# Experts' passes in another order, first gather by halves, last w2 and scatter by quarters, final mean on all partitions, one more prefetch tile

## The chip, the cores and the metric

One core of a Trainium2 chip runs the whole network. The metric is the time of one execution on the device in microseconds (us); lower is better. The engines are TensorE (PE, with its weight load PEld), VectorE (DVE), ScalarE (ACT), GpSimd (POOL) and SyncE (SP), whose queue issues nearly all transfers.

## The reference

256 tokens of width 1024 in float32 go through two blocks. Only the end of the second is touched here: a mixture of 32 experts, of which each token takes two, then a last norm and modulation.

```python
def hier_moe(h, w_rg, b_rg, w_re, b_re, w1e, w3e, w2e):
    pg = jax.nn.softmax((t @ w_rg + b_rg).astype(f32), axis=-1)
    pg_top, g_idx = lax.top_k(pg, 1)
    le = (t @ w_re + b_re).astype(f32).reshape(-1, N_GROUPS, EXPERTS_PER_GROUP)
    le_sel = jnp.take_along_axis(le, g_idx[:, :, None], axis=1)[:, 0]
    pe = jax.nn.softmax(le_sel, axis=-1)
    pe_top, e_idx = lax.top_k(pe, TOP_K)
    ...
    for e in range(N_EXPERTS):
        he = jax.nn.silu(t @ w1e[e]) * (t @ w3e[e])
        out = out + cw[:, e:e + 1] * (he @ w2e[e])
...
        x = x + gt2[:, None, :] * hier_moe(h2, ...)
    shf, scf = jnp.split(c_act @ w_ada_f + b_ada_f, 2, axis=-1)
    return modulate(rmsnorm_2(x, g_final), shf, scf)
```

## The kernel before

Activations lie with features on partitions: `x[0]` to `x[7]` are 128 features x 256 tokens each. The weights of all 32 experts are read, 96 MB in all: per expert two 1 MB halves of `w13` (512 input features each, w1 and w3 side by side) and 1 MB of `w2e`. Every load is one tile `we` of 128x2048 floats, issued by SP in the order of `expert_list` (L1838).

**The ring.** `expert_ring` collects 18 tiles from several pools: two `wa`, nine `we` (`NAHEAD`), three `s`, one `xl` and three `wf`, of which the later ones come free only when earlier stages are done with them. Load i takes the tile of load i-18, and SP issues loads strictly in order: a load whose tile is still read holds all that stand behind it. `expert_ahead` issues the 18 first loads as soon as their tiles are free. Loads of passes' experts below `NFIX` are of fixed experts; others read the expert's number from `moe_idx` (L1854), which the router's counts give, sorted so that the experts with most tokens come early.

**The passes.** `PASSES` (L41) lists eleven: six of two experts with 64 token slots each, then five of four experts with 32. One pass is `up` (tokens times `w13`, in two halves h), `mid` (transposes), `down` (times `w2e`) and, one pass later, `scatter` into four PSUM banks. `gather` picks the tokens of two passes at a time with one-hot matmuls out of `hhi`, `hlo` (tokens on partitions) into eight tiles `gT`. `moe_round` runs gather 0, the turn of the sort (`turn`), `up(0)`, `place`, and then for each n `up(n+1)`, `mid(n)`, `scatter(n-1)`, `down(n)`. The list of loads follows that only in part: it has `dn[2]` ahead of `up[3]`, while PE does `up(3)` ahead of `down(2)`.

**The start.** `post2` feeds the mean of squares of the tokens (`sums_tok`, matmuls with `mean1`); `moe` turns it into the scale `rt` (`rsqrt_tok`: add on DVE, power -0.5 on POOL), makes the router's choice in some thirty small DVE operations, counts slots with matmuls of `moe_msk`, builds the one-hots `oh` and starts gather 0. `keep_warm` puts matmuls on PE whose result nobody reads.

**The end.** The last pass's four `w2e` tiles come in two halves each (L1862), the first halves of all four first. After the last scatter `xr` (the residual x) takes up the sums, ACT squares it (`sq`), matmuls with `mean1` give the mean per token on partitions (128x2), DVE and POOL turn it into `rte`, four matmuls with the identity (`con`) spread it over all partitions (`bcast`, L444), and eight multiplies and eight modulations give `o`, which SP stores in five pieces.

Of the kernel before, what the change touches and what calls it, by code (L numbers as in the profile page):

```python
# [42 lines left out]
X_POOL, X_ORDER, X_ADD = (1, 2), (0, 3, 1, 2, 4, 5, 6, 7), (4, 6)  # L43
X_LOADS = (0, 1), (2, 3, 4), (5, 6, 7), ()
WARM = 40, 14
NEARLY = 2
NAHEAD = 9
# [134 lines left out]
class Net:  # L182
# [49 lines left out]
    def mm(self, out, lhsT, rhs, start=True, stop=True):  # L232
        self.nc.tensor.matmul(out, lhsT, rhs, start=start, stop=stop, skip_group_check=True)  # L233
# [26 lines left out]
    def setup(self):  # L260
# [29 lines left out]
        nc.vector.memset(self.mean1, 1.0 / D)  # L290
        self.ones = self.cst.tile([P, P], BF, name="ones")
        nc.gpsimd.memset(self.ones, 1.0)
        self.mhalf = self.cst.tile([P, 32], F32, name="mhalf")
        nc.gpsimd.memset(self.mhalf, -0.5)
# [137 lines left out]
    def sums_tok(self, srcs, out, start=True):  # L432
        for i, src in enumerate(srcs):
            for j in range(2):
                self.mm(out[:, j:j + 1], src[:, j * P:(j + 1) * P], self.mean1, start and i == 0 and j == 0, i == len(srcs) - 1)

    def rsqrt_tok(self, src, eps, n, tag="rt"):
        t = self.tmp(tag + "t", (P, n))
        e = self.tmp(tag + "e", (P, n))
        self.ts(t, src, eps, op0=OP.add)  # L440
        self.tt(e, t, self.mhalf[:, :n], OP.pow, eng=self.nc.gpsimd)
        return e
# [618 lines left out]
    def block2_in(self):  # L1061
# [13 lines left out]
        self.tt(e12, m3, self.mhalf[:, :2], OP.pow, eng=nc.gpsimd)  # L1075
# [23 lines left out]
    def block2(self, post):  # L1099
        nc, A = self.nc, self.A  # L1100
        rest = self.block2_in()
        with self.tc.tile_pool(name="b2", bufs=1, reuse_waits="tile") as bp:
# [50 lines left out]
            self.sums_tok(self.acc["n"][:2], self.pr[:, 128:130], False)  # L1153
# [424 lines left out]
    def moe_pre(self):  # L1578
# [13 lines left out]
        self.ei, self.e4 = T("ei", (P, 1)), T("e4", (P, 4))  # L1592
        tm = self.tmp("t3")[:, 0:P].rearrange("p (q e) -> p q e", e=32)
# [32 lines left out]
    def keep_warm(self, n):  # L1626

        p, a = self.spare
        for _ in range(n):
            self.mm(p[:, :S], a[:, 0:P], a)  # L1630

    def moe(self, final):
        nc, A = self.nc, self.A
        pr = self.pr
        self.sums_tok(self.acc["n"][2:], pr[:, 128:130], False)
# [6 lines left out]
        with self.tc.tile_pool(name="moe", bufs=1, reuse_waits="tile") as mp:  # L1642
# [61 lines left out]
            self.keep_warm(WARM[0])  # L1704
# [5 lines left out]
            self.mm(pk[:, 64:96], self.ones, mk[:, 32:64], False, True)  # L1710
            self.keep_warm(WARM[1])
# [3 lines left out]
            self.rk, self.cw = self.rc[:, 0:2], self.rc[:, 2:4]  # L1715
# [4 lines left out]
            def low(g, j):  # L1720
                c = slice(g * 512, (g + 1) * 512)
                self.stt(self.hlo[j][:, c], self.pt[g][j], rt[:, j:j + 1], self.hhi[j].bitcast(F32)[:, c], op0=OP.mult, op1=OP.subtract)
# [6 lines left out]
            self.tt(self.rk.rearrange("p a b -> p (a b)"), pk[:, 0:64], big, OP.add)  # L1729
# [5 lines left out]
            self.yl = self.wl.tile([P, D], F32R, tag="l", name="yl")  # L1735

            es = ExitStack()
            es.enter_context(self.tc.issue_after(picked.ins))
            gd, ge = t(2, 4), t(2, 4)
            self.tt(gd, lg, bc(gm, 4), OP.subtract)  # L1740
            self.act(ge, gd, AF.Exp)
            gs = red(ge, (2,), OP.add)
            d12, ds = t(8), t(2, 4)
            self.tt(d12, m2, m1, OP.subtract)
            self.tt(f2(ds), d12, f2(ohg), OP.mult)
            d1 = red(ds, (2,), OP.add)
            e2, dn, dn2, w1, w2 = t(2), t(2), t(2), t(2), t(2)
            self.act(e2, d1, AF.Exp)
            self.ts(dn, e2, 1.0, op0=OP.add)
            self.tt(dn2, dn, gs, OP.mult)  # L1750
            nc.vector.reciprocal(w1, dn2)
            self.tt(w2, w1, e2, OP.mult)
            for j in range(2):
                a = t(32)
                c = slice(32 * j, 32 * j + 32)
                self.ts(a, f2(o1m)[:, c], w1[:, j:j + 1], op0=OP.mult)
                self.stt(self.cw[:, j], f2(o2m)[:, c], w2[:, j:j + 1], a)
            cm = red(pk[:, 64:96], (1,))
            th, nx = t(3), t(1)
            for i in range(3):  # L1760
                self.ts(th[:, i:i + 1], cm, 64 * (i + 1) + 0.5, op0=OP.is_gt)
            order = self.expert_order(T, pk[:, 64:96])
            tn = t(3)
            for i in range(3):
                self.ts(tn[:, i:i + 1], self.top8[:, NWIDE - NFIX:NWIDE - NFIX + 1], 1024 * (i + 1) + 0.5, op0=OP.is_gt)
            self.tt(th, th, tn, OP.max)
            nc.vector.tensor_reduce(nx, th, axis=AX.X, op=OP.add)
            nxi = T("nxi", (P, 1), I32)
            nc.vector.tensor_copy(nxi, nx)
            es.close()  # L1770

            self.moe_round(*order)
            final()
            n_more = nc.values_load(nxi[0:1, 0:1], min_val=0, max_val=3)
            with self.tc.For_i(0, n_more, 1):
                self.ts(self.rk, self.rk, -64.0, op0=OP.add)
                for c, cap in ((slice(0, NWIDE), 64.0), (slice(NWIDE, NEXP), 32.0)):
                    a = self.rcP[:, 0:2, c]
                    self.ts(a, a, -cap, op0=OP.add)
                self.one_hot(0)  # L1780
                self.moe_round()
                final()

    def expert_order(self, T, cnt):
# [7 lines left out]
        rcT = rcT[:, 0:P]  # L1792
        ex = T("ex", (P, 32), BF)
# [5 lines left out]
        w = self.tmp("t2")  # L1799
# [9 lines left out]
        def turn():  # L1809
            self.po = self.bank("p1")  # L1810
# [27 lines left out]
    def expert_list(self):  # L1838
# [35 lines left out]
    def one_hot(self, b):  # L1874

        of = PASSES[2 * b:2 * b + 2]
        p0, n, cap = of[0][0], sum(q[1] for q in of), of[0][2]
        rk = self.rcP[:, 0:2] if b else self.rk
        self.oh[b] = [self.ptmp(f"oh{j}", (P, S), F32R, bufs=2) for j in range(2)]
        for j in range(2):  # L1880
            last = self.tt(self.oh[b][j][:, :n * cap].rearrange("p (e s) -> p e s", s=cap), self.C("iota")[:, 0:cap].unsqueeze(1).to_broadcast([P, n, cap]),
                           rk[:, j, p0:p0 + n].unsqueeze(2).to_broadcast([P, n, cap]), OP.is_equal)
        return last

    def moe_round(self, turn=lambda: None, place=lambda: None):
# [3 lines left out]
        ohs, gTs, hes, mids = self.oh, {}, {}, {}  # L1889

        def gather(b):
# [4 lines left out]
            gT = gTs[b] = [self.xp.tile([P, S], F32, tag=f"xh{k}", name=self.name("gT")) for k in range(KD)]  # L1896
            for dd in range(4):
# [6 lines left out]
                self.act(gT[2 * dd][:, :w], pg[:, 0:w], AF.Identity, bias=self.M(3)[:, 2 * dd:2 * dd + 1])  # L1904
                self.ts(gT[2 * dd + 1][:, :w], pg[:, S:S + w], self.M(3)[:, 2 * dd + 1:2 * dd + 2], op0=OP.add)

        def up(n):

            gT, (p, m, cap) = gTs[n // 2], PASSES[n]
            ph = self.bank("p1")  # L1910
            for h in range(2):
                w = self.expert_get(*[(0, p + i, h) for i in range(m)])
                for k in range(4):
                    for i in range(m):
                        c = n % 2 * P + i * cap
                        self.mm(ph[i * cap:(i + 1) * cap, :], gT[4 * h + k][:, c:c + cap], w[i][:, k * 512:(k + 1) * 512], h == 0 and k == 0, h == 1 and k == 3)
            s, he = self.tmp("t0"), self.tmp("t1")
            self.act(s, ph[:, 0:S], AF.Silu)
            self.tt(he, s, ph[:, S:2 * S], OP.mult)
            hes[n] = he  # L1920
# [268 lines left out]
```

## Time and profile before

| | us |
|---|---|
| median of 3 runs | 1623.12 (1621.87 to 1624.07) |
| the profiled execution | 1623.47 |
| its span | 1621.6 |

| engine | busy us | share of the span |
|---|---|---|
| PE | 1540.0 | 95% |
| PEld | 1360.5 | 84% |
| DVE | 1049.3 | 65% |
| ACT | 697.2 | 43% |
| POOL | 321.3 | 20% |

The profile is of one execution; its time is 1.9 us above its span and 0.35 us above the median. The chain of work that ended last is 76% PE over the whole span, but that is a mean over stages: the experts' stage takes the last sixth, and there the DMA engines move about 420 GB/s. The page shows the span in 40 slices; the rows of the experts' stage are those from about 1355 us on.

### The profile page before, as it was taken

The page shows a single profiled execution, that of the slowest core. Times are in us where ns is not written, and L with a number is a line of the kernel's source. Part 1 is how long each engine was busy: PE and PEld are TensorE (multiplying, and loading weights), DVE is VectorE, ACT ScalarE, POOL GpSimd, SP SyncE. Part 2 cuts the span into 40 slices and gives each one's busy share as a digit, 9 for nine tenths or more (in the row PEclk, how much of TensorE's full clock was granted, in tenths as well). Part 3 has the DMA queues.
Part 4 walks back from the last instruction along what each step waited for, and adds up shares of the span by engine and source line. Part 5 has one row for each costly group of instructions (what it writes and reads, how often), then busy time and mean ns, then how long its engine had stood idle before and what let it go on. Part 6 is the DMA issues. An engine that isn't in the chain of part 4 may idle for free.

```text
span 1621.6 us, 29873 instructions
## 1 busy us (share of the span) xinstructions
PE 1540.0 (95%) x11888; PEld 1360.5 (84%) x11888; DVE 1049.3 (65%) x1932; ACT 697.2 (43%) x1240; POOL 321.3 (20%) x340
## 2 busy tenths in 40 slices
PE   8999998999999999999999999998999989999885
PEld 8999996789999999999779999998889888454322
DVE  6777777776775577766986777757784576222112
ACT  6544444545444445444554445534464433111002
POOL 4122222132221112211222221224212031000000
PEclk9999999999999999999999999999999999999997
DMA  8676554135764567654324775543441087889993
GB/s 303 247 276 205 189 205 166 53 124 206 268 228 166 205 222 270 221 176 169 134 104 157 259 261 211 180 153 118 143 148 53 27 292 305 322 335 420 421 421 133
DMA packets 61330, 344.33 MB, mean 212 GB/s; under 512 B 11008, under 2 KB 15232, under 8 KB 27392
## 3 DMA queue, kind: packets, MB, share of 16 engines
q1 hardware_dynamic: 58368, 340.65, 57.0%
q0 software_dynamic: 640, 1.57, 0.4%
q8 instruction: 95, 1.56, 0.4%
q10 hardware_dynamic: 2176, 0.13, 0.1%
q14 instruction: 51, 0.42, 0.1%
HBM read 339.05 MB, written 2.36 MB: 211 GB/s over the span
## 4 chain that ended last, share of the span: by engine, by line
PE 76%; DVE 8%; DMA 8%; issue 3%; POOL 2%; ACT 2%; SPq 0%; ACTq 0%; DVEq 0%; POOLq 0%
PE ps L233 75%; DMA we<-in_w 5%; DMA we<-in_w2e 2%; DVE l L239 2%; PE ps L236 1%; ACT h L258 1%; DVE t L239 1%; POOL rte L239 1%; DVE xl L248 1%; DVE xh L243 0%; POOL t L239 0%; DMA s<-in_ev_win 0%; DVE t L248 0%; POOL sq L239 0%; POOL kne L239 0%
## 5 line engine op out<-in xcount | busy, mean ns | idle before, releaser
L233 PE MATMUL ps<-xh,h 128*128 128x256 f32 x1992 | 570.0, 286 | 12.3 <-ACT h L258 7.5
L233 PE MATMUL ps<-xh,l 128*128 128x256 f32 x1992 | 569.5, 286 | 0.2 <-DVE l L239 0.2
L233 PE MATMUL ps<-xl,h 128*128 128x256 f32 x1992 | 568.8, 286 | 0.3
L258 ACT ACTIVATE h<-s 128x1024 fp32r<-128x1024 f32 (+4 forms) x419 | 401.7, 960 | 368.4 <-PE ps L233 288.9
L239 DVE TENSOR_TENSOR l<-s,h 128x1024 fp32r<-128x1024 f32 (+4 forms) x416 | 465.3, 1126 | 140.9 <-ACT h L258 139.5
L233 PEld LDWEIGHTS ps<-xh,h 128*128 128x128 f32 x1992 | 380.0, 191 | 17.1 <-ACT h L258 6.8
L233 PEld LDWEIGHTS ps<-xh,l 128*128 128x128 f32 x1992 | 380.1, 191 | 5.9 <-DVE l L239 2.0
L233 PEld LDWEIGHTS ps<-xl,h 128*128 128x128 f32 x1992 | 380.4, 191 | 1.7 <-DVE xl L248 1.1
L233 PE MATMUL ps<-ah,h 128*128 128x256 f32 x704 | 201.4, 286 | 0.0
L239 POOL TENSOR_TENSOR t<-t,t 128x256 f32<-128x256 f32 x93 | 120.4, 1294 | 399.4 <-DVE t L239 339.0
L233 PE MATMUL ps<-ah,l 128*128 128x256 f32 x704 | 199.3, 283 | 0.1
L233 PE MATMUL ps<-al,h 128*128 128x256 f32 x704 | 199.1, 283 | 0.0
L233 PEld LDWEIGHTS ps<-ah,l 128*128 128x128 f32 x704 | 134.9, 192 | 0.4 <-DVE l L239 0.3
L233 PEld LDWEIGHTS ps<-al,h 128*128 128x128 f32 x704 | 135.0, 192 | 0.0
L233 PEld LDWEIGHTS ps<-ah,h 128*128 128x128 f32 x704 | 134.9, 192 | 0.0
L233 PE MATMUL ps<-we,gT 128*32 128x512 f32 (+1 forms) x512 | 100.6, 620 | 10.1 <-DMA we<-in_w 9.7
L239 DVE TENSOR_TENSOR t<-ps,rb 128x256 f32<-128x256 f32 x196 | 81.9, 421 | 32.5 <-PE ps L233 24.8
L258 ACT ACTIVATE ah<-t 128x256 fp32r<-128x256 f32 x88 | 36.7, 417 | 115.5 <-POOL t L239 115.5
L233 PEld LDWEIGHTS ps<-we,gT 128*32 128x32 f32 (+1 forms) x512 | 26.7, 124 | 66.1 <-issue 46.0
L239 DVE TENSOR_TENSOR al<-t,ah 128x256 fp32r<-128x256 f32 x88 | 38.0, 431 | 62.9 <-ACT ah L258 62.9
L248 DVE SCALAR_TENSOR_TENSOR ada<-s,ca,ada 128x1024 f32<-128x1024 f32 x56 | 71.5, 1277 | 0.0
L239 POOL TENSOR_TENSOR sa<-sa,sq 128x256 f32<-128x256 f32 x34 | 41.8, 1231 | 149.9 <-ACT sq L258 149.4
(484 smaller groups left out, 2100.5 us busy)
## 6 DMA issues: line engine op xcount, KB each, us to landing
s<-in_ffn_gu SPq DMA_DIRECT2D x87, 1024.0 KB
we<-in_w SPq DMA_DIRECT2D x64, 1024.0 KB
s<-in_ffn_dn SPq DMA_DIRECT2D x64, 704.0 KB
we<-in_w2e SPq DMA_DIRECT2D x28, 1024.0 KB
s<-in_w_ada SPq DMA_DIRECT2D x24, 1024.0 KB
s<-in_w_in SPq DMA_DIRECT2D x18, 1024.0 KB
s<-in_w_ada_f SPq DMA_DIRECT2D x8, 1024.0 KB
s<-in_ev_win SPq DMA_DIRECT2D x7, 1024.0 KB
```

The costliest lines, as they stand in the source:

```text
L233: self.nc.tensor.matmul(out, lhsT, rhs, start=start, stop=stop, skip_group_check=True)
L236: self.nc.tensor.transpose(out, in_, ident)
L239: return (eng or self.nc.vector).tensor_tensor(out, a, b, op=op)
L248: self.nc.vector.scalar_tensor_tensor(out, a, s, b, op0=op0, op1=op1)
L258: self.nc.scalar.activation(out, a, f, **kw)
```

## The change

1. `PASSES` alternates: (0, 2, 4, 6) of two experts, (12, 16) of four, 8, 20, 10, 24, 28. `expert_list` now follows PE's order throughout: `up[n+1]`, then `dn[n]`. `NFIX` is 8 instead of 6.
2. `NAHEAD` is 10 instead of 9: 19 tiles in the ring. `dynamic_dma_scratch_size=8192` frees the memory. The two first expert loads are issued some 100 us earlier, beside loads of `w_in`.
3. The router: the last mean of squares is summed before the router's own matmuls of the last tile; slots are counted with one more matmul (`pre_skip`), so that `oh` is built straight from PSUM against `slots`, without the two steps `t<-moe_msk` and `moe_rc<-ps,t`. The fillers of `keep_warm` are 26 and 5 (and 6 new ones at the end) instead of 40 and 14.
4. Gather 0 is cut in halves: four `gT`, the first half of `up(0)`, the other four, the rest of `up(0)`. The sort and the weights' exponentials come after it.
5. The last `down` goes by quarters: its `w2e` tiles come in four pieces each (16 of 256 KB), and down, scatter and residual follow quarter by quarter. `w2e` is laid out for that in memory.
6. The final mean: eight matmuls of `mean1` broadcast with `sq` (128x256) leave the mean of squares on all partitions; DVE adds the epsilon, POOL takes the power -0.5 of all 128x256 values (`t1<-t0,mhalf`), and the multiplies read that. The two adds of squares on DVE, the two residual adds on POOL, and the spreading matmuls with `rte` are gone. `mhalf` is one column, broadcast.

```diff
-NFIX, NWIDE = 6, 12
-PASSES = [(p, 2, 64) for p in range(0, NWIDE, 2)] + [(p, 4, 32) for p in range(NWIDE, NEXP, 4)]
+NFIX, NWIDE = 8, 12
+PASSES = [(p, 2 if p < NWIDE else 4, 64 if p < NWIDE else 32) for p in (0, 2, 4, 6, 12, 16, 8, 20, 10, 24, 28)]
...
-WARM = 40, 14
+WARM = 26, 5, 6
-NAHEAD = 9
+NAHEAD = 10
...
-            self.sums_tok(self.acc["n"][:2], self.pr[:, 128:130], False)
+            self.summed = self.sums_tok(self.acc["n"], self.pr[:, 128:130], False)
...
             self.mm(pk[:, 0:64], us, mk)
+            self.mm(pk[:, 0:64], self.skip, mk, False, False)
...
-            big = t(64)
-            self.ts(big, mk, -1.0e6, 1.0e6, op0=OP.mult, op1=OP.add)
...
-            self.tt(self.rk.rearrange("p a b -> p (a b)"), pk[:, 0:64], big, OP.add)
             picked = self.one_hot(0)
...
-        return up[0] + up[1] + dn[0] + up[2] + dn[1] + dn[2] + up[3] + sum((u + d for u, d in zip(up[4:], dn[3:])), []) + dn[-1]
+        return up[0] + sum((u + d for u, d in zip(up[1:], dn)), []) + dn[-1]
...
-                for c in range(2):
+                for c in range(4):
                     for o, a in self.late:
-                        self.nc.sync.dma_start(o[:, c * D:(c + 1) * D], a[:, c * D:(c + 1) * D])
+                        self.nc.sync.dma_start(o[:, c * 512:(c + 1) * 512], a[:, c * 512:(c + 1) * 512])
...
-        gather(0)
+        gather(0, (0, 1))
+        up_half(0, 0)
+        gather(0, (2, 3))
+        turn, place = early() if early else (lambda: None, lambda: None)
         turn()
-        up(0)
+        up_half(0, 1)
         place()
...
-            down(n)
-        scatter(N - 1)
...
+            if n < N - 1:
+                down(n)
+        w = None
+        for q in range(5):
+            if q < 4:
+                w, last = down(N - 1, q * 256, (q + 1) * 256, w)
+            if q:
+                with self.tc.issue_after(last.ins):
+                    scatter(N - 1, (2 * q - 2, 2 * q - 1))
+                for d in (2 * q - 2, 2 * q - 1):
+                    self.stt(self.x[d], acc[q - 1][:, (d % 2) * S:(d % 2 + 1) * S], self.M(5)[:, d:d + 1], self.x[d])
...
-        for k in X_ADD:
-            self.tt(sq[k], sq[k], sq[k + 1], OP.add)
-        self.sums_tok([q for k, q in enumerate(sq) if k - 1 not in X_ADD], p)
-        pb = self.bcast(self.rsqrt_tok(p[:, :2], EPS, 2), "p0")
+        with self.tc.issue_after(self.downed.ins):
+            for k in range(KD):
+                self.mm(p[:, :S], self.mean1.to_broadcast([P, P]), sq[k], k == 0, k == KD - 1)
+        ms, r = self.tmp("t0"), self.tmp("t1")
+        self.ts(ms, p[:, :S], EPS, op0=OP.add)
+        self.tt(r, ms, self.mhalf.to_broadcast([P, S]), OP.pow, eng=self.nc.gpsimd)
...
-            self.tt(ok, self.x[k], pb[:, :S], OP.mult)
+            self.tt(ok, self.x[k], r, OP.mult)
...
-    nc = bacc.Bacc("TRN2", target_bir_lowering=False, num_devices=1)
+    nc = bacc.Bacc("TRN2", target_bir_lowering=False, num_devices=1, dynamic_dma_scratch_size=8192)
```

On PE, at the end of gather 0, before: the last gather matmul (`hlo`), the two matmuls of the sort, and the first half of `up(0)` (`we,gT`), whose eight matmuls read the two first tiles of the ring.

```order
L233 MATMUL ps_17011<-oh_3167_16916,hlo_16908 128x256
L233 LDWEIGHTS ones
L233 MATMUL ps_17022<-moe_ex,ones 128x32
L236 MATMUL ps_17022<-con,moe_rc 128x128
L233 MATMUL ps_17027<-we_15207,gT_16970 64x512
L233 MATMUL ps_17027<-we_15209,gT_16970 64x512
```

The same place now, after the sixteenth gather matmul of thirty-two:

```order
L233 MATMUL ps_16930<-oh_3168_16898,hlo_16891 128x256
L233 MATMUL ps_16941<-we_15207,gT_16911 64x512
L233 MATMUL ps_16941<-we_15209,gT_16911 64x512
L233 MATMUL ps_16941<-we_15207,gT_16912 64x512
L233 MATMUL ps_16941<-we_15209,gT_16912 64x512
L233 MATMUL ps_16941<-we_15207,gT_16913 64x512
L233 MATMUL ps_16941<-we_15209,gT_16913 64x512
L233 MATMUL ps_16941<-we_15207,gT_16914 64x512
L233 MATMUL ps_16941<-we_15209,gT_16914 64x512
L233 MATMUL ps_16950<-oh_3167_16897,hhi_16888 128x256
```

The first half of `up(0)` moved ahead of half of the gather and ahead of the sort's two matmuls.

On SP's queue, before, the last loads that need no index, and the first that read `moe_idx` (load 18, which takes the tile of load 0):

```order
L1864 DMA we_16808<-in_w2e 128x2048
L1864 DMA we_16810<-in_w2e 128x2048
L1864 DMA we_16812<-in_w2e 128x2048
L1854 TENSOR_LOAD moe_idx
L1854 ISA x2
L1864 ISA
L1864 DMA we_17223<-in_w 128x2048
```

The same place now:

```order
L1874 DMA we_16818<-in_w 128x2048
L1874 DMA we_17212<-in_w 128x2048
L1874 DMA we_17313<-in_w2e 128x2048
L1874 DMA we_17315<-in_w2e 128x2048
L1864 TENSOR_LOAD moe_idx
L1864 ISA x2
L1874 ISA
L1874 DMA we_17332<-in_w 128x2048
```

There were 18 loads ahead of the first index; now there are 22, and of these the last three (`we_17212`, `we_17313`, `we_17315`) reuse tiles.

On PE, at the end of the program, before: the last scatter, the means per token, and the spreading of `rte`.

```order
L233 MATMUL ps_16969<-t_3449_18677,yh 128x256
L233 MATMUL ps_16969<-t_3449_18677,yl 128x256
L233 MATMUL ps_18795<-mean_170,sq_18804 128x1 x2
L233 MATMUL ps_18795<-mean_170,sq_18808 128x1 x2
L233 MATMUL ps_18830<-con,rte_18827 128x128 x2
```

The same place now:

```order
L233 MATMUL ps_16910<-t_3448_18624,yh 128x256
L233 MATMUL ps_16910<-t_3448_18624,yl 128x256
L233 MATMUL ps_18768<-yh 128x256 x6
L233 MATMUL ps_18775<-sq_18776,mean_170 128x256
L233 MATMUL ps_18775<-sq_18778,mean_170 128x256
L233 MATMUL ps_18775<-sq_18780,mean_170 128x256
```

Five more of that kind follow. Eight wide matmuls (after six fillers) stand where the small means stood, and PE has nothing to do after the power any more.

## Rows read from the trace of the kernel before

**Rows 1.** Busy by stretch: start:end, length, engines' busy time (instructions), clock, DMA share, GB/s.

```profile
1440.00:1590.00 150.00, 133.36 (x800) 57.15 (x800) 30.50 (x75) 17.54 (x33) 0.00 (x0) 0.98 1.01 420
```

**Rows 2.** The chain that ended last, the experts' passes: start, length, what.

```profile
1411.44 0.59 PE ps L236 x4
...
1441.44 0.58 PE ps L236 x4
...
1482.99 20.12 DMA we<-in_w
```

**Rows 3.** Busy by stretch of 5 us, up to where transfers are steady.

```profile
1355.00:1360.00 5.00, 5.00 (x45) 5.00 (x44) 0.84 (x2) 0.42 (x1) 0.15 (x1) 1.00 0.45 187
...
1370.00:1375.00 5.00, 3.82 (x27) 3.19 (x27) 4.93 (x28) 2.87 (x6) 0.00 (x0) 1.00 0.43 180
1375.00:1380.00 5.00, 2.92 (x16) 1.43 (x17) 3.41 (x18) 1.76 (x2) 0.00 (x0) 0.86 0.00 0
...
1425.00:1430.00 5.00, 5.00 (x43) 4.79 (x41) 2.45 (x7) 1.90 (x4) 0.00 (x0) 1.00 0.57 236
1430.00:1435.00 5.00, 5.00 (x29) 2.28 (x29) 2.58 (x7) 0.98 (x2) 0.00 (x0) 1.00 0.00 0
```

**Rows 4.** SP's queue in order of time: start, time from first to last, loads.

```profile
1360.08 4.16 SPq L1864 DMA_DIRECT2D we<-in_w2e  x4
1383.78 12.23 SPq L1864 DMA_DIRECT2D we<-in_w  x8
...
1417.55 1.58 SPq L1864 DMA_DIRECT2D we<-in_w2e  x2
1434.60 5.97 SPq L1864 DMA_DIRECT2D we<-in_w  x8
```

**Rows 5.** Busy by stretch of 2 us, where the last weights land.

```profile
1590.00:1592.00 2.00, 1.98 (x15) 0.39 (x7) 0.06 (x1) 0.69 (x1) 0.00 (x0) 1.00 0.69 279
```

**Rows 6.** Instructions in order of time, router and first gather: start, length, [idle before].

```profile
1360.78 0.42 ACT L258 ACTIVATE sq<-xr 128x256 f32<-128x256 f32 x1 [3.06 <-DVE xr L248]
...
1362.72 0.50 PE L233 MATMUL ps<-mean,sq 128*128 128x1 f32 x4
...
1369.28 0.76 DVE L239 TENSOR_TENSOR oh<-con,moe_rc 128x256 fp32r<-128x256 f32 x2
...
1378.03 0.18 PE L233 MATMUL ps<-moe_ex,ones 32*128 32x32 bf16 x1 [2.08 <-DVE moe_ex L243]
...
1378.40 8.78 PE L233 MATMUL ps<-we,gT 128*64 128x512 f32 x32
...
1387.99 7.09 PE L233 MATMUL ps<-we,gT 128*64 128x512 f32 x32 [0.38 <-DVE moe_rcP L1818]
```

**Rows 7.** Instructions in order of time, from the last down to the output.

```profile
1598.83 1.90 PE L233 MATMUL ps<-we,t 128*32 128x512 f32 x10
...
1600.83 0.69 ACT L258 ACTIVATE yh<-ps,cs 128x512 fp32r<-128x512 f32 x1 [3.74 <-PE ps L233]
...
1603.02 1.66 DVE L248 SCALAR_TENSOR_TENSOR xr<-ps,mod,xr 128x256 f32<-128x256 f32 x4 [0.71 <-PE ps L233]
1603.53 1.59 ACT L258 ACTIVATE sq<-xr 128x256 f32<-128x256 f32 x4 [2.02 <-DVE xr L248]
...
1609.22 2.74 DVE L239 TENSOR_TENSOR o<-xr,ps 128x256 f32<-128x256 f32 x8 [2.10 <-PE ps L233]
```

**Rows 8.** POOL by tile (min/median/max ns) and, last, by line (busy, mean ns).

```profile
L239 POOL TENSOR_TENSOR rte<-rtt,mhalf x10: 687/722/1787, 18.2 to 1607.2; 128x2 f32<-128x2 f32 x10
L239 POOL TENSOR_TENSOR kne<-knt,mhalf x4: 1007/1266/1985, 1105.4 to 1164.9; 128x4 f32<-128x4 f32 x4
...
L239 POOL TENSOR_TENSOR xr<-t,xr x2: 727/730/732, 1594.5 to 1595.6; 128x256 f32<-128x256 f32 x2
...
L1375 POOL COPY rw_wc<-W 128x4 f32<-128x4 f32 x4 | 1.6, 397 | 1.4 <-ACT W L258 1.4
```

**Rows 9.** Busy by stretch, where the two first expert loads go now.

```profile
1095.00:1100.00 5.00, 5.00 (x44) 5.00 (x43) 2.06 (x3) 2.35 (x4) 4.08 (x8) 1.00 0.39 127
```

More of the change, by code (lines that the diff above doesn't have):

```diff
@@ L232, in mm @@
     def mm(self, out, lhsT, rhs, start=True, stop=True):
-        self.nc.tensor.matmul(out, lhsT, rhs, start=start, stop=stop, skip_group_check=True)
+        return self.nc.tensor.matmul(out, lhsT, rhs, start=start, stop=stop, skip_group_check=True)
     def tr(self, out, in_, ident):
@@ L434, in sums_tok @@
             for j in range(2):
-                self.mm(out[:, j:j + 1], src[:, j * P:(j + 1) * P], self.mean1, start and i == 0 and j == 0, i == len(srcs) - 1)
+                last = self.mm(out[:, j:j + 1], src[:, j * P:(j + 1) * P], self.mean1, start and i == 0 and j == 0, i == len(srcs) - 1)
+        return last
     def rsqrt_tok(self, src, eps, n, tag="rt"):
+        e = self.tmp(tag + "e", (P, n))
         t = self.tmp(tag + "t", (P, n))
-        e = self.tmp(tag + "e", (P, n))
         self.ts(t, src, eps, op0=OP.add)
-        self.tt(e, t, self.mhalf[:, :n], OP.pow, eng=self.nc.gpsimd)
+        self.tt(e, t, self.mhalf.to_broadcast([P, n]), OP.pow, eng=self.nc.gpsimd)
         return e
@@ L1629, in keep_warm @@
         for _ in range(n):
-            self.mm(p[:, :S], a[:, 0:P], a)
+            last = self.mm(p[:, :S], a[:, 0:P], a[:, 0:S])
+        return last
     def moe(self, final):
@@ L1703, in moe @@
             mk = f2(msk)
-            self.keep_warm(WARM[0])
+            with self.tc.issue_after(self.summed.ins):
+                self.keep_warm(WARM[0])
             pk = self.bank("p1")
@@ L1747, in moe @@
[L1747 to L1767, printed above, removed]
@@ L1768, in moe, with weights @@
-            nxi = T("nxi", (P, 1), I32)
-            nc.vector.tensor_copy(nxi, nx)
-            es.close()
-            self.moe_round(*order)
+            nxi = T("nxi", (P, 1), I32)
+            def weights():
+                es = ExitStack()
+                es.enter_context(self.tc.issue_after(picked.ins))
+                self.ts(self.rc[:, 0:2].rearrange("p a b -> p (a b)"), pk[:, 0:64], BIG, op0=OP.add)
+                cm = red(pk[:, 64:96], (1,))
+                order = self.expert_order(T, pk[:, 64:96])
+                gd, ge = t(2, 4), t(2, 4)
+                self.tt(gd, lg, bc(gm, 4), OP.subtract)
+                with self.tc.issue_after(self.gathered.ins):
+                    self.act(ge, gd, AF.Exp)
+                gs = red(ge, (2,), OP.add)
+                d12, ds = t(8), t(2, 4)
+                self.tt(d12, m2, m1, OP.subtract)
+                self.tt(f2(ds), d12, f2(ohg), OP.mult)
+                d1 = red(ds, (2,), OP.add)
+                e2, dn, dn2, w1, w2 = t(2), t(2), t(2), t(2), t(2)
+                with self.tc.issue_after(self.gathered.ins):
+                    self.act(e2, d1, AF.Exp)
+                self.ts(dn, e2, 1.0, op0=OP.add)
+                self.tt(dn2, dn, gs, OP.mult)
+                nc.vector.reciprocal(w1, dn2)
+                self.tt(w2, w1, e2, OP.mult)
+                for j in range(2):
+                    a = t(32)
+                    c = slice(32 * j, 32 * j + 32)
+                    self.ts(a, f2(o1m)[:, c], w1[:, j:j + 1], op0=OP.mult)
+                    self.stt(self.cw[:, j], f2(o2m)[:, c], w2[:, j:j + 1], a)
+                th, nx, tn = t(3), t(1), t(3)
+                for i in range(3):
+                    self.ts(th[:, i:i + 1], cm, 64 * (i + 1) + 0.5, op0=OP.is_gt)
+                    self.ts(tn[:, i:i + 1], self.top8[:, NWIDE - NFIX:NWIDE - NFIX + 1], 1024 * (i + 1) + 0.5, op0=OP.is_gt)
+                self.tt(th, th, tn, OP.max)
+                nc.vector.tensor_reduce(nx, th, axis=AX.X, op=OP.add)
+                nc.vector.tensor_copy(nxi, nx)
+                es.close()
+                return order
@@ L1773, in moe @@
+            self.moe_round(weights)
+            self.spare = self.bank("p1"), self.yh
+            with self.tc.issue_after(self.scattered.ins):
+                self.keep_warm(WARM[2])
             final()
@@ L1895, in gather @@
             w = P * len(PASSES[2 * b:2 * b + 2])
-            gT = gTs[b] = [self.xp.tile([P, S], F32, tag=f"xh{k}", name=self.name("gT")) for k in range(KD)]
-            for dd in range(4):
+            if 0 in dds:
+                gTs[b] = [self.xp.tile([P, S], F32, tag=f"xh{k}", name=self.name("gT")) for k in range(KD)]
+            gT = gTs[b]
+            for dd in dds:
                 pg = self.bank("p0")
@@ L1903, in gather @@
                             self.mm(pg[:, o * S:o * S + w], hx[j][:, c], ohs[b][j][:, :w], o == 0 and j == 0 and i == 0, j == 1 and i == 1)
-                self.act(gT[2 * dd][:, :w], pg[:, 0:w], AF.Identity, bias=self.M(3)[:, 2 * dd:2 * dd + 1])
-                self.ts(gT[2 * dd + 1][:, :w], pg[:, S:S + w], self.M(3)[:, 2 * dd + 1:2 * dd + 2], op0=OP.add)
-        def up(n):
[L1909 to L1920, printed above, removed]
+                for o in range(2):
+                    k = 2 * dd + o
+                    if o == 0 or b == 0 and dd == 0:
+                        self.gathered = nc.scalar.activation(gT[k][:, :w], pg[:, o * S:o * S + w], AF.Identity, bias=self.M(3)[:, k:k + 1])
+                    else:
+                        self.ts(gT[k][:, :w], pg[:, o * S:o * S + w], self.M(3)[:, k:k + 1], op0=OP.add)
@@ new lines, in up_half @@
+        def up_half(n, h):
+            gT, (p, m, cap) = gTs[n // 2], PASSES[n]
+            if h == 0:
+                phs[n] = self.bank("p1")
+            ph = phs[n]
+            w = self.expert_get(*[(0, p + i, h) for i in range(m)])
+            for k in range(4):
+                for i in range(m):
+                    c = n % 2 * P + i * cap
+                    self.mm(ph[i * cap:(i + 1) * cap, :], gT[4 * h + k][:, c:c + cap], w[i][:, k * 512:(k + 1) * 512], h == 0 and k == 0, h == 1 and k == 3)
+            if h:
+                s, he = self.tmp("t0"), self.tmp("t1")
+                self.act(s, ph[:, 0:S], AF.Silu)
+                self.tt(he, s, ph[:, S:2 * S], OP.mult)
+                hes[n] = he
```

108 lines of the change are left out of this document (50 added, 58 removed).

## The prediction

> **What bounds the kernel now.** I read the view by stretches first, because the page's 76% of PE is a mean over stages. From 1440 to 1590 us the DMA engines' share is 1.01 at 420 GB/s while PE is busy 133.4 of 150 us [rows 1]: the weights' transfers are the limit, and one MB (1.049 million bytes) takes 1.049/420 = 2.50 us. The chain of waits says the same. Up to about 1460 it runs through the PE, two two-expert passes in 1441.44 - 1411.44 = 30.0 us; after that it is made of transfers, in pieces of eight MB such as the one of 20.12 us [rows 2]. So the end of the kernel is: when the last weight lands, plus what has to be done with it afterwards.
>
> Two questions follow. Where do transfers pause before the last weight? The stretches of 5 us show it [rows 3]: a share of 0.45 in 1355 to 1360, 0.43 in 1370 to 1375 and none in the next five, 0.57 in 1425 to 1430 and none in the next five. SP's queue shows why [rows 4]: it issues nothing between 1360.08 + 4.16 and 1383.78, nor between 1417.55 + 1.58 and 1434.60. The loads there wait for tiles that the PE still reads. And when does the last weight land? In 1590 to 1592 the share is 0.69 [rows 5]; at full share that is 1.35 us, so it lands at 1591.35. The span ends at 1621.6, 30.25 us later.
>
> **The start (step 4, part of 3).** Load 18 takes the tile that the first half of `up(0)` reads, so SP issues it when that half is done, at 1383.78 [rows 4]. Three things move ahead of that point [rows 6]. The mean's matmuls stood behind the router's own until 1362.72, though `sq` was done at 1360.78 + 0.42 = 1361.2; they can start 0.1 later, which is 1.3 to 1.4 us saved, taken as 1.3. The one-hots then start at 1369.28 - 1.3 = 1368.0; the two DVE steps taken out I count as nothing, and the added matmul too, since it stands among four short ones. From the one-hots to the end of gather 0 went 1375.95 - 1369.28 = 6.67 us (the PE's idle of 2.08 before 1378.03 begins at 1375.95); half the gather is 3.35. Two evictions of about 0.42 (a quarter of the 1.66 for four PSUM reads of that shape [rows 7]) come before the half of `up` can go on: 0.85. The half itself is half of 7.09, 3.55; before, it took 1383.78 - 1378.40 = 5.38, because PE's clock was granted at 0.86 in that stretch, a mean between its levels of 1.2 and 2.4 GHz, after its idle [rows 3]. Sum: 1368.0 + 3.35 + 0.85 + 3.55 = 1375.75, so SP issues about **8.0 us** earlier. The sort, which now comes later, delays nobody there: the three loads that go next need no index (NFIX), and the tiles for the ones after come free only with the second half.
>
> **The list (step 1).** The pause of 1425 to 1435 is 0.43 x 5 + 5 = 7.2 us [rows 3]. It comes from the order: SP waits for the tile of `dn[2]`, which PE frees only after `up(3)`, while `up(3)`'s own tiles, free earlier, stand behind it in the queue. With the list in PE's order each tile is the next that comes free. PE frees 12 tiles in 30.0 us [rows 2], 2.50 us each, exactly what a MB takes; so in the two-expert passes neither waits long, and in the four-expert passes PE frees twice as many. I leave 1.5 us of the pause and count **5.7 us**; bounds are 7.2 and 0. Alternating the passes has no other price: PE has 150 - 133.4 = 16.6 us of slack in that stretch [rows 1].
>
> **One more tile (step 2).** The 19th load fits into the pause of 1355 to 1360, 0.55 x 5 = 2.75 us [rows 3], which exists because SP waits for the `xl` tile until 1360.08 [rows 4]. One MB less comes after the restart. The two loads moved to about 1095 add 2 MB where the share is 0.39 and PE is busy throughout [rows 9]; counted as nothing, at worst 2 x 2.5 us if loads of `w_in` behind them on SP came too late for PE.
>
> **The last landing.** Before, 78 MB took 1591.35 - 1383.78 - 7.2 = 200.4 us, 2.57 each with latency. Now 77 x 2.57 = 197.9 after 1375.8, and 1.5 of pause: 1575.2, that is **16.2 us** earlier (8.0 + 2.6 + 5.7, rounded).
>
> **The tail (steps 5 and 6).** Before: 9.4 us from the landing to the end of the last down matmuls (1598.83 + 1.90 = 1600.73), 8.5 to the first `o` at 1609.22, 12.4 to the end [rows 7]. PE lost the 9.4 because the matmuls of the last halves stood in its queue among scatters and means that waited for ACT and POOL. Now the quarters follow each other. After the last piece lands, one quarter's matmuls remain: 0.19 each at 512 columns [rows 7], eight at half width 0.8, with the drain 1.0. Then the chain: from `yh` to `xr` was 1603.02 - 1600.83 = 2.19 at 512 columns, taken as 1.9; two `xr` at 0.42 are 0.83; the last `sq` 0.40; mean matmul and add 0.9 together; hand-overs 0.3. That is 4.4 us, then the power, X, then the 12.4 of multiplies and stores, unchanged. Smaller pieces of the last 4 MB could cost up to 1 us; not counted. New tail: 17.8 + X, against 30.25.
>
> **X, the power of 128x256 values on POOL**, is the one price that the trace does not show. The nearest row by engine and shape is the add of 128x256, 0.73 us; the nearest by operation is the power of 128x2, at least 0.69 us [rows 8]. I take the sum, 1.4, as if columns streamed. The other end is steep: the power of four columns takes at least 1.007, so 0.16 us for each further column, and 0.687 + 254 x 0.16 = 41.3 us for 256. Against such a line speaks the copy of 128x4, 0.40 us, more than half the 256-column add: here a small form says little of a wide one. I lean to the shape, but keep 0.73 and 41.3 as bounds.
>
> **Sum.** 1623.47 - 16.2 - (30.25 - 17.8) + X = 1594.8 + X in the profiled execution's terms. That execution is 0.35 above the median, so the median would be 1594.5 + X; with X = 1.4, **1596 us**.
>
> **Rivals.**
> A, slower: the power costs what the step from two to four columns says. For it: the two minima are steady. Against it: the add and the copy above. Time: 1594.5 + 41.3 = 1636. It decides from X = 28.6, or 0.11 us per column. The Trainium skill, GPSIMD Engine Reference (sections 3.1 and 7), describes such an instruction as a loop over elements, about 2.6 cycles each for two inputs, and charges four cycles per element for every link of a dependent chain; the add's row agrees with the first, and a power made of a long chain would be this rival. No row here has a power wider than four columns.
> B: one of the two gains in transfers isn't had. If the first tile comes free as late as before (evictions or the sort hold PE), +8.0: 1604. If PE's jitter keeps the pause, +5.7: 1602. For it: the PE frees tiles no faster than the DMA fills them [rows 2].
> C: the power lies between, 5 to 22 us: 1600 to 1616.
>
> **How the numbers follow.** The forecast with X up to 5 gets 0.48 and spans 1590 (X 0.73, no pause left, start and tail each 1 to 2 us better) to 1600; B 0.13; C 0.18; X between 22 and 35, around no change, 0.03; A 0.18. Taking 1590 to 1616 holds the first three, 0.79. About 0.2%, 3.2 us, is what a measurement of this kernel can tell from no change. Faster by more: 0.48 + 0.13 + 0.18 = 0.79; within 0.03; slower 0.18.
>
> **What would show it.** SP's first load after the ring's fill near 1375.8; no pause of SP over 2 us after it; the last weight near 1575; PE's last down within 1 us of it; the first `o` 4.4 + X later; and POOL's one row of a 128x256 power. If that row is above 28.6 us, the sign is wrong whatever else holds; if the last weight lands at 1580 or later, B.

## The result, and the profile after

| | us |
|---|---|
| before, median of 4 runs | 1623.01 (1621.87 to 1624.07) |
| after, median of 4 runs | 1641.93 (1640.34 to 1642.98) |
| ratio | 1.0116, 95% interval 1.0098 to 1.0133 |
| profiled execution of after, its span | 1642.62, 1640.9 |

The kernel got 1.2% slower; the forecast was 1.7% faster. One row says why. This is POOL by tile in the kernel after (minimum, median, maximum ns), to be held against [rows 8]:

```profile
L239 POOL TENSOR_TENSOR kne<-knt,mhalf x4: 1008/1252/1985, 1106.5 to 1165.8; 128x4 f32<-128x4 f32 x4
...
L239 POOL TENSOR_TENSOR t<-t,mhalf x1: 41127/41127/41127, 1587.6 to 1587.6; 128x256 f32<-128x256 f32 x1
```

The power of 128x256 values takes 41.1 us, and the end of the program in order of time (start, length, engine, [idle before]) shows that nothing stands beside it:

```profile
1579.48 1.07 PE L233 MATMUL ps<-we,t 128*32 128x256 f32 x16
...
1580.57 0.81 ACT L258 ACTIVATE sq<-xr 128x256 f32<-128x256 f32 x2 [0.94 <-DVE xr L248]
...
1581.28 0.46 ACT L258 ACTIVATE yh<-ps,cs 128x256 fp32r<-128x256 f32 x1
...
1583.48 3.61 PE L233 MATMUL ps<-sq,mean 128*128 128x256 f32 x16
1587.13 0.43 DVE L243 TENSOR_SCALAR t<-ps 128x256 f32<-128x256 f32 x1 [3.29 <-PE ps L233]
1587.64 41.13 POOL L239 TENSOR_TENSOR t<-t,mhalf 128x256 f32<-128x256 f32 x1 [223.22 <-DVE t L243]
1628.80 2.97 DVE L239 TENSOR_TENSOR o<-xr,t 128x256 f32<-128x256 f32 x8 [41.24 <-POOL t L239]
```

Against [rows 7], the multiplies `o` start at 1628.80 instead of 1609.22. Take the power out and they would start at 1587.7, 21.5 us earlier than before: the rest of the change is a gain, as forecast, but a smaller one (the forecast without the power was 1575.2 + 5.4 = 1580.6, which is 28.6 earlier). Busy time by stretch (length, engines' busy time, clock, DMA share, GB/s) shows the transfers of the kernel after, against [rows 3, 5]:

```profile
1370.00:1385.00 15.00, 15.00 (x74) 7.86 (x74) 9.35 (x48) 5.51 (x10) 0.00 (x0) 0.91 0.64 236
1385.00:1410.00 25.00, 25.00 (x133) 11.91 (x128) 7.93 (x21) 4.05 (x8) 0.00 (x0) 1.00 0.85 339
1410.00:1440.00 30.00, 30.00 (x201) 14.89 (x200) 9.30 (x24) 5.42 (x10) 0.00 (x0) 1.00 1.01 421
...
1400.00:1405.00 5.00, 5.00 (x26) 1.65 (x24) 1.59 (x3) 1.38 (x2) 0.00 (x0) 1.00 0.28 79
...
1576.00:1578.00 2.00, 2.00 (x28) 1.07 (x24) 0.95 (x3) 0.95 (x2) 0.00 (x0) 1.00 0.87 316
```

The pause of 1425 to 1435 is gone, a new one of 0.72 x 5 = 3.6 us stands at 1400 to 1405, and the last weight lands at 1577.8 instead of 1591.5 (here and below the landing is read from stretches of 1 us, the bytes left at the end taken at the rate before it; that is good to about 0.1 us). The first column behind the length is PE's busy time: 15, 25 and 30 us of 15, 25 and 30. In these stretches transfers pause and PE doesn't. What holds them at 1400 is seen in SP's loads (first two rows) and PE's matmuls (third):

```profile
1391.48 0.33 SPq L1874 DMA_DIRECT2D we<-in_w  x1
...
1402.70 0.33 SPq L1874 DMA_DIRECT2D we<-in_w  x1
...
1399.07 3.60 PE L233 MATMUL ps<-we,t 128*64 128x512 f32 x16
```

The load at 1402.70 takes the tile of the first `w2e`, which `down(0)` reads, and PE comes to `down(0)` only after gather 1, which runs from 1391.38 to 1396.6, and the first matmuls of `up(2)`.

### The profile page after: what moved, and what is told of

It is laid out like the page before. It is cut to its first block, busy times and chain, and to the rows that moved or that the text cites. A ratio compares the mean times of both kernels' runs of the same rounds, so it can differ in the third digit from the quotient of the medians.

```text
span 1640.9 us, 29888 instructions
## 1 busy us (share of the span) xinstructions
PE 1530.8 (93%) x11892; PEld 1359.1 (83%) x11892; DVE 1049.1 (64%) x1938; ACT 696.9 (42%) x1241; POOL 362.3 (22%) x338
## 4 chain that ended last, share of the span: by engine, by line
PE 69%; issue 15%; DVE 8%; POOL 4%; ACT 2%; DMA 1%; SPq 0%; ACTq 0%; DVEq 0%; POOLq 0%
PE ps L233 68%; POOL t L239 3%; DVE l L239 2%; PE ps L236 1%; ACT h L258 1%; DVE xl L248 1%; DVE t L239 0%; POOL rte L239 0%; DVE xh L243 0%; DMA s<-in_ev_win 0%; DVE t L248 0%; POOL sq L239 0%; POOL kne L239 0%; DVE x L239 0%; DMA x<-in_xT 0%
## 5 line engine op out<-in xcount | busy, mean ns | idle before, releaser
L233 PE MATMUL ps<-xh,h 128*128 128x256 f32 x1992 | 570.2, 286 | 12.1 <-ACT h L258 7.3
L239 POOL TENSOR_TENSOR t<-t,mhalf 128x256 f32<-128x256 f32 x1 | 41.1, 41127 | 223.2 <-DVE t L243 223.2
```

The source lines that it names most:

```text
L233: return self.nc.tensor.matmul(out, lhsT, rhs, start=start, stop=stop, skip_group_check=True)
L239: return (eng or self.nc.vector).tensor_tensor(out, a, b, op=op)
```

## The experiments

The kernel's stages before the experts end up to 7 us earlier or later in one execution than in another: over the twelve profiled executions, one of each kernel, the add of `rtt` starts between 1358.15 and 1365.31. So where a place in the trace is compared, it is counted from SP's load into the `xl` tile, which waits for the last step of the stage before (1360.08 before, 1360.95 after). A spread is left even so: in the seven executions whose ring, list and pieces are those of after, the last weight lands 215.7 to 217.1 us behind that load, and a difference of less than 1.4 us in this place says nothing.

### What the power costs, and where

`e1_mean_per_token`: the final mean put back.

```diff
-            for k in range(KD):
-                self.mm(p[:, :S], self.mean1.to_broadcast([P, P]), sq[k], k == 0, k == KD - 1)
-        ms, r = self.tmp("t0"), self.tmp("t1")
-        self.ts(ms, p[:, :S], EPS, op0=OP.add)
-        self.tt(r, ms, self.mhalf.to_broadcast([P, S]), OP.pow, eng=self.nc.gpsimd)
+            self.sums_tok(sq, p)
+        r = self.bcast(self.rsqrt_tok(p[:, :2], EPS, 2), "p0")[:, :S]
```

> The changed kernel with only the final mean put back: mean per token (128x2), power of 128x2 on POOL, spread by matmuls with the identity. Theory 1 (the 41.1 us of the 128x256 power are the whole loss, the rest of the change is a gain): the power's 41.1 us go, the eight wide mean matmuls (3.6 us) give way to sixteen small ones (1.9), and add, small power and spreading come back (some 2.3 us), so 1641.9 - 41.1 - 1.7 + 2.3 = 1601 us, clearly faster than before. Theory 2 (the rest of the change gains nothing, because other waits took its place): 1615 to 1623 us.

Measured: 1604.4 us, ratio to before 0.988 (0.9847 to 0.9912). The whole loss sits in the final mean; all else that the change does is worth 1.2%. The time is 3.4 us above the 1601 of theory 1: the sixteen small mean matmuls took 5.76 us, not the 1.9 that had been counted.

`e2_before_wide_mean`: the reverse, the kernel before with the wide mean alone (`self.mhalf[:, 0:1].to_broadcast([P, S])` as exponent).

> The kernel before with only the new final mean: wide mean matmuls and the power of 128x256 on POOL. Theory 1: nothing covers the power at the end, so 1623 + 41.1, less the small power and the spreading (1609.22 - 1606.96 = 2.3 us), plus some 1 us of wider mean matmuls: about 1663 us. Theory 2 (the power is that slow only in the changed kernel, through what runs beside it): under 1630 us.

Measured: 1662.4 us where before had 1621.5, ratio 1.0236 (1.0202 to 1.027). The power takes 41.14 us there too, so nothing else in the change makes it slow:

```profile
1608.27 41.14 POOL L239 TENSOR_TENSOR t<-t,mhalf 128x256 f32<-128x256 f32 x1 [10.34 <-DVE t L243]
```

`e3_pow_pieces`: the power in four pieces, the last with an exponent tile written out.

```diff
-        self.tt(r, ms, self.mhalf.to_broadcast([P, S]), OP.pow, eng=self.nc.gpsimd)
+        half = self.tmp("t2")
+        self.nc.gpsimd.memset(half[:, 0:96], -0.5)
+        for a, e, dense in ((0, 16, 0), (16, 64, 0), (64, 160, 0), (160, 256, 1)):
+            self.tt(r[:, a:e], ms[:, a:e], half[:, 0:e - a] if dense else self.mhalf.to_broadcast([P, e - a]), OP.pow, eng=self.nc.gpsimd)
```

> The changed kernel with its power cut into four pieces of 16, 48, 96 and 96 columns, the last with an exponent tile that is written out instead of one broadcast column. Theory 1 (0.16 us per column and some 0.4 us fixed): 2.9, 8.0, 15.6 and 15.6 us, time within 2 us of the changed kernel's. Theory 2 (the broadcast exponent makes it slow): the last piece under 2 us, the others as above. Theory 3 (a wide form passes into some other, faster or slower, regime): the pieces don't lie on a line.

Measured: 1643.3 us in the one execution that was taken. POOL by tile, minimum, median and maximum of the pieces with 16, 48 and 96 columns, and then the last piece in order of time:

```profile
L239 POOL TENSOR_TENSOR t<-t,mhalf x3: 2895/7999/15623, 1587.1 to 1597.9; 128x16 f32<-128x16 f32 x1, 128x48 f32<-128x48 f32 x1, 128x96 f32<-128x96 f32 x1
...
1613.53 15.65 POOL L239 TENSOR_TENSOR t<-t,t 128x96 f32<-128x96 f32 x1
```

The points lie on a line: (41.127 - 2.895)/240 = 0.159 us per column and 0.35 us fixed. At two and four columns that line gives 0.66 and 0.98, where the rows of before had 0.69 and 1.007. The exponent's form makes no difference (15.62 and 15.65). The power is paid per column, from 2 columns to 256. The Trainium skill, GPSIMD Engine Reference, section 3.1, describes an elementwise instruction as a loop over elements; the line agrees. Its figure of about 2.6 cycles per element for two inputs stands beside the measurement of an add; it is not a price of this power.

`e4_sqrt_reciprocal`: a root on ACT, its table loaded ahead, and a reciprocal on DVE.

```diff
+        z = self.tmp("t0")
+        nc.gpsimd.memset(z[:, 0:1], EPS)
+        self.act(z[:, 1:2], z[:, 0:1], AF.Sqrt)
+        self.eps1 = z[:, 0:1]
...
-        ms, r = self.tmp("t0"), self.tmp("t1")
-        self.ts(ms, p[:, :S], EPS, op0=OP.add)
-        self.tt(r, ms, self.mhalf.to_broadcast([P, S]), OP.pow, eng=self.nc.gpsimd)
+        r = self.tmp("t1")
+        self.act(r, p[:, :S], AF.Sqrt, bias=self.eps1)
+        self.nc.vector.reciprocal(r, r)
```

> The changed kernel with the power replaced by a square root on ACT (its table loaded ahead, beside the last down) and a reciprocal on DVE, both 128x256. Theory 1: 1641.9 - 41.1, less the add (0.4) that the square root takes in, plus about 0.5 for the root and between 0.4 and 2 for the reciprocal: 1601 to 1603 us. If the wide mean is itself the trouble (PE matmuls, waits), it stays above 1610.

```profile
1585.24 0.48 ACT L258 ACTIVATE t<-ps,t 128x256 f32<-128x256 f32 x1 [2.84 <-PE ps L233]
1585.75 1.75 DVE L2035 RECIPROCAL t<-t 128x256 f32<-128x256 f32 x1 [3.80 <-ACT t L258]
1587.54 2.97 DVE L239 TENSOR_TENSOR o<-xr,t 128x256 f32<-128x256 f32 x8
```

Those are its steps in order of time: 2.3 us to the first `o` in place of 41.7. Measured 1601.1 us, ratio 0.9866 (0.9832 to 0.9901). The wide mean itself is no trouble: the time is not above that of `e1_mean_per_token`. The runs below start from this kernel (their diffs leave out what they share with it).

### Where the gain in transfers comes from

`e5_old_list`: order of passes and list of loads as before.

```diff
-PASSES = [... for p in (0, 2, 4, 6, 12, 16, 8, 20, 10, 24, 28)]
+PASSES = [... for p in (0, 2, 4, 6, 8, 10, 12, 16, 20, 24, 28)]
...
-        return up[0] + sum((u + d for u, d in zip(up[1:], dn)), []) + dn[-1]
+        return up[0] + up[1] + dn[0] + up[2] + dn[1] + dn[2] + up[3] + sum((u + d for u, d in zip(up[4:], dn[3:])), []) + dn[-1]
```

> The kernel with square root and reciprocal (1601.1 us), with the order of passes and the list of loads as they were before (NFIX stays 8, 19 tiles). Theory 1 (the list in PE's order took away the pause): SP's pause of 10 us and more ahead of the loads of pass 4 comes back, the last weight lands some 5.7 us later, 1606 to 1607 us. Theory 2 (the 19th tile alone did it): within 1.5 us of 1601.

Measured: 1606.4 us, ratio 0.9891 (0.9863 to 0.992). The last weight lands 223.3 us after the `xl` load, in `e4_sqrt_reciprocal` 216.7: 6.6 us later. By time alone the two can't be told apart (0.9866 with 0.9832 to 0.9901). The pause is back, at a place some 5 us earlier in this execution (busy by stretch, share and GB/s last):

```profile
1420.00:1425.00 5.00, 5.00 (x32) 2.95 (x32) 2.71 (x10) 1.12 (x2) 0.00 (x0) 1.00 0.32 134
1425.00:1430.00 5.00, 5.00 (x26) 1.72 (x24) 1.34 (x2) 0.69 (x1) 0.00 (x0) 1.00 0.62 215
```

The shares lack (0.68 + 0.38) x 5 = 5.3 us there, and SP issues nothing between 1412.5 and 1425.8; theory 1 holds. The order of the passes and the list of loads went back together, so which of the two it is was not shown.

`e6_whole_gather`: gather 0 in one piece ahead of `up(0)` (in the trace one matmul of `up(0)` still stands ahead of the gather's last eight).

```diff
-        gather(0, (0, 1))
-        up_half(0, 0)
-        gather(0, (2, 3))
+        gather(0)
         turn, place = early() if early else (lambda: None, lambda: None)
         turn()
-        up_half(0, 1)
+        up(0)
```

> The kernel with square root and reciprocal (1601.1 us), with gather 0 in one piece ahead of up(0), sort and all else unchanged. Theory 1 (the half gather frees the first tile earlier and that moves the last landing): SP's first load into a reused tile comes 3 to 4 us later, the last weight too, 1604 to 1605 us. Theory 2 (the transfers lose that time again at the tiles that come free next): SP's load later, the last landing within 1 us, 1601 us.

Measured: 1600.4 us, ratio 0.9852 (0.9828 to 0.9876). The last weight lands 216.9 us after the `xl` load, with halves 216.7: theory 2 holds, and the half gather is worth nothing. SP's queue after the restart (start, time from first to last, loads), first with halves (`e4_sqrt_reciprocal`, `xl` load at 1359.33), then whole (1357.30):

```profile
1375.72 5.88 SPq L1874 DMA_DIRECT2D we<-in_w2e  x2
1383.07 7.20 SPq L1874 DMA_DIRECT2D we<-in_w  x5
```

```profile
1375.76 0.33 SPq L1874 DMA_DIRECT2D we<-in_w  x1
1376.61 3.33 SPq L1874 DMA_DIRECT2D we<-in_w2e  x2
1381.35 7.45 SPq L1874 DMA_DIRECT2D we<-in_w  x5
```

Counted from `xl`, the restart is at 16.0 with halves (its first load, at 1375.3, stands just ahead of these rows) and at 18.5 whole. But the next loads of `in_w` come at 23.7 and 24.0, nearly the same, since they wait for tiles that the second half of `up(0)` frees, and so does the second `in_w2e` of these rows (1381.27 and 1379.61). The three stretches of 15, 25 and 30 us in `e6_whole_gather` (length, PE busy first, share and GB/s last) answer to those of after above:

```profile
1366.00:1381.00 15.00, 15.00 (x70) 8.10 (x72) 9.06 (x48) 5.51 (x10) 0.00 (x0) 0.89 0.51 192
1381.00:1406.00 25.00, 25.00 (x132) 11.66 (x129) 7.98 (x22) 4.04 (x8) 0.00 (x0) 1.00 0.92 364
1406.00:1436.00 30.00, 30.00 (x202) 14.89 (x201) 9.23 (x25) 5.42 (x10) 0.00 (x0) 1.00 1.01 422
```

15 x 192 + 25 x 364 + 30 x 422 is 24.6 million bytes; with halves, 15 x 236 + 25 x 339 + 30 x 421 is 24.6 as well. What the first stretch loses, the second has back.

`e7_nine_ahead`: `NAHEAD = 9`, 18 tiles.

> The kernel with square root and reciprocal (1601.1 us), with 18 tiles in the ring instead of 19. Theory 1: one MB more is left after the restart, the last landing and the time 2.5 us later, 1603.6 us. Theory 2 (in the two-expert passes PE and transfers are even, so a tile less lets both wait more often): 4 us or more later, 1605 us and above. Theory 3: nothing, since the first loads wait for other tiles anyway.

Measured: 1603.9 us, ratio 0.9867 (0.9836 to 0.9897). By time alone that can't be told from `e4_sqrt_reciprocal`; by place the last weight lands 219.4 us after the `xl` load instead of 216.7: 2.7 us, about what one tile was to bring (2.5).

### The tail

`e8_mean_in_quarters`: squares and mean matmuls issued quarter by quarter.

```diff
+                if q > 1:
+                    self.mean_of(2 * q - 4, self.scattered)
                 for d in (2 * q - 2, 2 * q - 1):
                     self.stt(self.x[d], acc[q - 1][:, (d % 2) * S:(d % 2 + 1) * S], self.M(5)[:, d:d + 1], self.x[d])
+                    self.square(d)
...
```

> The kernel with square root and reciprocal (1601.1 us), with squares and mean matmuls issued inside the quarters instead of all eight at the end (there they took 3.62 us, of which only the last two squares' need to come last). Expected: the stretch from the last down to the multiplies gets 1.5 to 2.5 us shorter, 1599 us. If the wide matmuls get in the way of the quarters' scatters, the gain goes back: 1601.

From the last landing to the first `o`: 10.4 us instead of 11.5. Ratio 0.9832 (0.9805 to 0.9858), 1598.8 us: faster than both kernels, though by time not told from `e4_sqrt_reciprocal`. Less came than was expected, since mean matmuls now stand ahead of the last quarter's down, which starts 2.5 us after the landing instead of 1.6.

`e9_halves`: last `w2e` loads, down and scatter by halves, from `e4_sqrt_reciprocal`.

```diff
-                for c in range(4):
+                for c in range(2):
                     for o, a in self.late:
-                        self.nc.sync.dma_start(o[:, c * 512:(c + 1) * 512], a[:, c * 512:(c + 1) * 512])
+                        self.nc.sync.dma_start(o[:, c * D:(c + 1) * D], a[:, c * D:(c + 1) * D])
...
-        for q in range(5):
-            if q < 4:
-                w, last = down(N - 1, q * 256, (q + 1) * 256, w)
+        for q in range(3):
+            if q < 2:
+                w, last = down(N - 1, q * 512, (q + 1) * 512, w)
...
```

> The kernel with square root and reciprocal (ratio to before 0.987), with the last w2e loads, down and scatter by halves instead of quarters. Theory 1 (the quarters shorten what is left after the last landing): the stretch from the last landing to the first o, 11.4 us with quarters, gets 2 to 4 us longer. Theory 2 (that stretch is a chain of ACT, DVE and PE steps that goes on from the quarter before, not from the landing): it changes by less than 1 us.

From the last landing (1578.7) to the first `o`: 12.9 us instead of 11.5, less than the 2 to 4 of theory 1 and more than theory 2 allows. The last weight lands 215.9 us after the `xl` load instead of 216.7. That alone is within the spread, but larger pieces do move faster, and by the rates below the last 4.19 MB should land 0.6 us sooner (10.2 us instead of 10.9; an estimate). Five us of the last pieces, by halves and then by quarters (`e4_sqrt_reciprocal`); the last column is GB/s:

```profile
1572.00:1577.00 5.00, 5.00 (x35) 2.93 (x34) 2.50 (x5) 1.38 (x2) 0.00 (x0) 1.00 1.02 409
```

```profile
1570.00:1575.00 5.00, 5.00 (x54) 3.36 (x52) 2.22 (x6) 1.17 (x2) 0.00 (x0) 1.00 1.05 386
```

Net, by place, quarters would be worth some 0.6 us, less than the spread; the times (ratios 0.9865 and 0.9866) show no difference. Before, this stretch took 17.7 us; most of the way down to 11.5 is there with halves already, so it doesn't hang on the quarters.

`e10_no_fillers`: `e8_mean_in_quarters` without the six filler matmuls.

> The kernel with squares and means inside the quarters (ratio 0.983), without the six filler matmuls at the end. Theory 1 (they stand in front of the last means on PE): the last means end 0.5 to 1 us earlier. Theory 2 (they keep PE's clock up): PE's clock falls to its lower level there and the means take longer, 1 us later or more. The whole time moves by at most 1 us either way.

Measured: 1599.5 us, ratio 0.9846 (0.9826 to 0.9867); last landing to first `o` 10.3 us instead of 10.4. In that kernel the fillers do nothing. In the kernel after they run for 0.7 us right ahead of the eight mean matmuls (1582.77 to 1583.48), whose first squares were done by then; leaving them out there was not run. PE's clock in the kernel without them, third column from the end, is granted at its upper level of 2.4 GHz up to the end of the last matmuls:

```profile
1575.00:1580.00 5.00, 4.97 (x42) 3.61 (x38) 2.91 (x7) 2.88 (x8) 0.00 (x0) 1.00 0.00 0
...
1581.00:1582.00 1.00, 0.74 (x4) 0.34 (x2) 0.00 (x0) 0.22 (x1) 0.00 (x0) 1.00 0.00 0
```

## Why the prediction was wrong

**The step that failed is X.** It took 1.4 us for the power of 128x256, "as if columns streamed", and measured 41.13. The trace held the answer: the rise from two to four columns in [rows 8] gave 0.16 us per column and 41.3 us in all, within 0.2 us of the row after. (It is the two minima that give it; by the medians, 0.722 and 1.266, it would have been 0.27 per column and 70 us.) What led away from it was the argument that the copy of 128x4, at 0.40 us, shows that a small form says little of a wide one. That compares another operation. At four columns the copy takes 0.40 and the power 1.007; at 256 the add takes 0.73 and the power 41.13. Two widths of the same operation give its fixed cost and its cost per column, and the add's 0.73 us bounds only an operation that costs as little per column as an add. Rival A, with its place, its price and its point of decision (28.6 us), was the right mechanism, and its time of 1636 us is 6 below the measured one.

**The remaining 6 us** are the rest of the sum: 1641.93 - 41.13 = 1600.8 against 1594.5. By place, 1.7 us of them are the last landing and 4.4 the tail, 0.3 came back at the very end, and the rest, 0.5, is where the two profiled executions stood (the `xl` load 0.9 later, and 0.7 above the median instead of 0.35).

- *Last landing, forecast 16.2 us earlier.* Counted from the `xl` load, it is 231.4 us before and 216.9 after: 14.5. The tile brought 2.7 (forecast 2.6), the list 6.6 (5.7), so what is left for the start is 5.2 (8.0); each of these is a difference of single executions, good to 1.4 us. SP's restart was as forecast: 7.8 us earlier (23.7 to 15.9 after the `xl` load). The step that failed there is the one that carried this over to the last landing. Only two loads go at the restart (1376.85 and 1377.27), not three: the third takes a tile that the second half of `up(0)` reads and goes at 1382.82, the next at 1384.61. And the pause comes back at 1400 to 1405 as 3.6 us where 1.5 were left. Taking the half gather away cost nothing. In these stretches PE is busy without a break; that fits PE's whole work up to the four-expert passes setting how many tiles come free, so that moving a release within it shifts a pause. Some 0.7 of the 2.8 that is missing is the price of smaller pieces, which the prediction named and did not count (an estimate: 4.19 MB at 406 GB/s before and 380 after). Which parts of the start make up the rest (the sort behind the gather, the wait of 2.08 us that is gone, the clock, granted at 0.73 in 1370 to 1375) was not taken apart.
- *The mean of the router, forecast 1.3.* From the `xl` load to the add of `rtt` it went 3.18 before and 2.52 after: 0.7. The mean's last matmuls did run 1.1 us earlier (2.64 and 1.50 after the `xl` load), but the add began only when the router's own matmuls, which now stand behind them and write the same PSUM tile, were done:

```profile
1362.45 0.50 PE L233 MATMUL ps<-mean,sq 128*128 128x1 f32 x4
1362.81 0.61 PE L233 MATMUL ps<-pre_wr,b_u 128*128 128x36 f32 x4
...
1363.47 0.16 DVE L243 TENSOR_SCALAR rtt<-ps 128x2 f32<-128x2 f32 x1 [1.51 <-PE ps L233]
```

That SP's restart came as forecast all the same is luck: the path from that add to the first `oh`, whose two DVE steps fewer had been counted as nothing, gave 0.55 (6.02 us before, 5.47 after).

- *The two loads moved to about 1095, counted as nothing.* From SP's store of x ahead of them to the powers `kne` behind them it took 18.1 us before and 18.5 after; the other runs spread from 17.6 to 18.7. No cost is seen: right.
- *The tail, forecast 5.4 us from the landing to the power.* It took 9.8 (1577.8 to 1587.64; rows of the first section). PE finished the last quarter 2.7 us after the landing instead of 1.0: busy without a break since 1570, it still had the third quarter's down and the second's scatter ahead of it.

```profile
1577.82 1.07 PE L233 MATMUL ps<-we,t 128*32 128x256 f32 x16
...
1578.82 0.39 PE L233 MATMUL ps<-t,yh 128*128 128x256 f32 x1
```

From there it took 7.1 instead of 4.4: `yh` waited for two squares on ACT, and all eight mean matmuls, 3.61 us, came after the last scatter, where 0.9 had been counted for mean and add together.
- *From the first `o` to the end* 12.1 us, forecast 12.4. Right.

Rival B had the right suspicion (a gain in transfers that PE takes back), at a smaller price: 2.8 of the 8.0, not all. Rival C did not occur.

## What to carry to other kernels

A price per column is read from two widths of the same operation, by their minima, and it is believed until a row contradicts it; a row of another operation at the wanted width is no contradiction. If a change puts an operation with no cover at the end of the program, its worst price decides the sign, so that one has to be known first. And where transfers wait for buffers that a busy engine frees, an earlier first release can move the pause and not the end, as here: compare bytes moved over the whole stretch.

## What was not expected of the hardware

POOL's power costs 0.159 us per column of 128 values, up to 256 columns, with 0.35 us fixed, whatever the exponent's form. DVE's reciprocal of 128x256 took 1.75 us, four times the 0.43 of the add of the epsilon on that shape. Pieces of 256 KB moved at 374 to 386 GB/s and pieces of 512 KB at 409, against 420 for 1 MB. The Trainium skill, DMA: Bandwidth & Descriptors, section Bandwidth, advises at least 1 MiB for each transfer; the direction agrees, and with several transfers in flight the loss here is 8 to 11% at a quarter of that size.
